# Nineteen pairs of input projections as Strassen pairs behind the head, with z and half of the conv branch kept in DRAM

## The chip, the cores and the metric

The kernel runs on one core of a Trainium2 chip. The metric is the device time of one execution in microseconds. Five engines work beside each other, each on its own list of instructions: TensorE (PE, matmuls), VectorE (DVE), ScalarE (ACT), GpSimd (POOL) and SyncE (SP, which issues loads). ACT and POOL issue DMAs too.

## The reference

One layer of a hybrid trunk over 1024 frames of width 1024, in float32: a modulated norm, one input projection that feeds a short-convolution branch, a Mamba-2 branch and the branch gates, then a squared-ReLU MLP and a final norm. Cut to what the change touches:

```python
u = rms_norm(x, ln1) * (1 + scale1) + shift1       # scale, shift, gate: (silu(c) @ w_ada + b_ada)
gl, cb, cc, cx, z, xbc, dt = split(u @ w_in)       # 2048, 3 x 1024, 2048, 4096, 32 columns
p_conv = (cb * causal_conv(cc * cx, conv_w)) @ w_conv_out            # 3 taps
xs, bs, cs = split(silu(causal_conv(xbc, ssm_conv_w) + ssm_conv_b))  # 4 taps
dt = softplus(dt + dt_bias); a = -exp(a_log) * dt
y = ssd_scan(xs * dt, a, bs, cs) + d_skip * xs     # within a chunk: scores * exp(a_cum[t] - a_cum[s]), s <= t
y = group_rms_norm(y * silu(z)) * ssm_norm_w       # 8 groups of 256 channels
mix = (sigmoid(gl0) * p_conv + sigmoid(gl1) * (y @ w_ssm_out)) @ w_o
x = x + gate1 * mix
u2 = rms_norm(x, ln2) * (1 + scale2) + shift2
x = x + gate2 * (square(relu(u2 @ w_up)) @ w_down)
return rms_norm(x, final_norm)
```

## The kernel before, in words

Everything is kept transposed: channels on 128 partitions, the 1024 frames in two halves of 512 columns. A float32 product is made of three matmuls in a rounded float type: the weight tile is split into `whi` (ACT, L87) and `wlo` (DVE, L41), the activations likewise (`uh`, `ul`), and `mm3` adds hi x hi, hi x lo and lo x hi. `proj` makes one tile of 128 output channels: 8 blocks of the inner dimension x 2 halves x 3 = 48 matmuls of 128x512, in two of the four banks of PSUM in pool `mm`. `strassen_pair` makes two tiles at once by seven half-size products, 84 matmuls; it needs sums of quarters of the activations (`tops`, T1 to T4) and of the weights (`s12`, `s34` on DVE), and holds all four banks.

The stages in order:
- the head: the norm of x, the first products with w_ada (`gemv`, one custom DVE instruction over 128x1024 and a short read), and the first four gate tiles, as the parts of u come
- gate tiles 4 to 15 (`gl`, sent to `gl_d` in DRAM) by `proj`, with the remaining 32 products with w_ada (`wada2`, loaded by SP into four buffers) on DVE beside them, and the dt block: 32 matmuls with `wd`, a chain of some 25 small operations on DVE (softplus as a series, the names `ev`, `den`, `z2`) and the cumulative sums `acum` by matmuls with `tri`
- eight groups: `proj_group(g)` makes four xbc tiles (two `xs`, `bf`, `cf`, each with a causal convolution of four taps in `cacc` on DVE) and two z tiles; `ssd_group(g)` runs the scan over eight chunks of 128 frames. A chunk has four transposes and scores (A), the decay `seg` (on DVE: subtract and min, then ACT's Exp), the products B, and the state C. After the last chunk POOL multiplies `xs` by `zs` and stores it to `y_d`, and the sum of squares goes through a split (`sqh`, `sql`) to a matmul (again named C) and a row copy
- the conv branch: eight times c, x and b tiles by `proj`, and three taps
- the products with w_conv_out, w_ssm_out and w_o, the second norm, and up: four tiles by `proj`, fourteen Strassen pairs, each hid tile stored to `hid_d`
- down: hid tiles are read back on POOL's queue (`hr`), split, and multiplied.

The order on each engine is set when the program is built: a scheduler places the instructions by their dependences, the buffers of the pools (`mm` four banks, `cacc` and `raw` two each, two sets `p2g` of xs, bf, cf) and the order of the code. An engine then runs its list in that order, and waits on semaphores where the list says so.

Of the kernel before, what the change touches and what calls it, by code (L numbers as in the profile page):

```python
# [35 lines left out]
def hybrid_trunk(tc, xT, par, hrows, crow, wada1, wada2, win, wdt, wco, wso, wo, wup, wdn, out):  # L36
# [188 lines left out]
    hb = d0.tile([P, 32], F32, name="hb")  # L225

    with tc.tile_pool(name="p0", bufs=2) as p0, tc.tile_pool(name="p0x", bufs=1) as p0x, \
            tc.tile_pool(name="ps0", bufs=2, space=PSUM) as ps0:
# [8 lines left out]
        sp.dma_start(prm, par)
        for h in (0, 1):
            ps = mm.tile([P, H], F32, name="mm")
            pe.matmul(ps, lhsT=ones[0:1, :], rhs=crw[:, hs[h]], start=True, stop=True)  # L240
            act.activation(ct[:, hs[h]], ps, AF.Tanh, scale=0.5)
            stt(cb[:, hs[h]], ct[:, hs[h]], 1.0, ps, ALU.add, ALU.mult)

        xt = [[p0x.tile([P, H], F32, name=f"x{k}{h}") for h in (0, 1)] for k in range(KT)]
        wa = {}

        def load_ada(j):
            for q in (1, 0):
                wa[j, q] = p0.tile([P, T], F32, name="wada", bufs=4)
                sp.dma_start(wa[j, q], wada1[j, :, q])  # L250

        for h in (0, 1):
            for k in range(KT):
                sp.dma_start(xt[k][h], xT[k, :, hs[h]])
        load_ada(0)

        wps = mm.tile([P, H], F32, name="mm")

        def gemv(w_, o, eng):
            if eng is dve:  # L260
                dve.tensor_tensor_reduce(out=w_, in0=w_, in1=cb, scale=0.5, scalar=prm[:, BADA + o:BADA + o + 1],  # L261
                                         op0=ALU.mult, op1=ALU.add, accum_out=mcol[:, o:o + 1])
# [525 lines left out]
```

## Time and profile before

| What | Value |
|---|---|
| Time, median of 3 runs | 2224.09 us (2221.95 to 2225.82) |
| The profiled execution | 2224.57 us, its span 2222.8 us |
| Mean granted TensorE clock | 0.986 |
| Busy PE, DVE, ACT, POOL | 98%, 60%, 31%, 9% of the span |
| DMA | 249.72 MB, mean 112 GB/s |

Busy shares are of the whole span, over stages that differ. Lines of a timeline read: start in us, duration, engine, line of the code, operation, output and input with their sizes, how many in a row, and in brackets how long the engine had been idle and what ended that. L41, L44, L47, L87 and L93 are lines of small helpers (`tt`, `stt`, `tsc`, `load_w`, `split`), so that tiles and not lines tell such instructions apart.

### The profile page before, as it was taken

The numbers are of one execution on the slowest core, as the hardware profiler recorded it, in microseconds if no ns is written. First come the engines' busy times: TensorE is split into PE (matmuls) and PEld (weight loads), VectorE is DVE, ScalarE is ACT, GpSimd is POOL, SyncE is SP. The second block draws the span as 40 slices with busy tenths as digits, with TensorE's granted clock in tenths as the row PEclk, the third lists the DMA queues.
The fourth block names the chain that finished last, engine by engine and source line by source line (L and its number), as shares of the span: only waits on it lengthen the run. The fifth ranks groups of instructions, "written<-read, shape, count | busy, mean of one in ns | idle before, by whom it ended". The sixth has DMA issues, their size and how long they took to land.

```text
span 2222.8 us, 26082 instructions
## 1 busy us (share of the span) xinstructions
PE 2169.0 (98%) x10158; PEld 1779.9 (80%) x10158; DVE 1332.8 (60%) x2195; ACT 693.9 (31%) x1044; POOL 189.4 (9%) x208
## 2 busy tenths in 40 slices
PE   5899999999999999999999999999999998999998
PEld 3778888888888888888888878888888886888887
DVE  8951368768678877574323477746755545544444
ACT  4322223333334333232111211234544443211122
POOL 5100001010110101101000000021000001000003
PEclk6999999999999999999999999999999999999999
DMA  7763222222222222231114475453233337332202
GB/s 248 269 236 116 76 57 65 79 72 71 76 59 82 77 68 84 62 83 58 49 48 154 154 231 171 152 199 109 90 110 108 114 114 256 103 109 92 86 29 77
DMA packets 105070, 249.72 MB, mean 112 GB/s; under 512 B 9281, under 2 KB 44481, under 8 KB 104946
## 3 DMA queue, kind: packets, MB, share of 16 engines
q1 hardware_dynamic: 86866, 191.22, 27.0%
q0 software_dynamic: 11584, 41.95, 5.1%
q10 hardware_dynamic: 6496, 14.88, 2.1%
q8 instruction: 80, 1.31, 0.2%
q14 instruction: 44, 0.36, 0.1%
HBM read 205.87 MB, written 42.14 MB: 112 GB/s over the span
## 4 chain that ended last, share of the span: by engine, by line
PE 80%; issue 12%; DVE 5%; DMA 2%; POOL 1%; ACT 0%; SPq 0%; POOLq 0%; DVEq 0%
PE mm L105 24%; PE mm L102 24%; PE mm L103 24%; PE B L469 2%; PE B L474 2%; DVE x L44 1%; PE C L491 1%; DVE wada L261 1%; POOL hid_d L668 1%; PE A L446 1%; DMA wada<-in_wada 1%; DVE ul L44 1%; DMA yr<-y_d 0%; PE st L190 0%; PE A L447 0%
## 5 line engine op out<-in xcount | busy, mean ns | idle before, releaser
L103 PE MATMUL mm<-ul,whi 128*128 128x512 f32 x1376 | 543.4, 395 | 4.8 <-DVE ul L44 4.6
L102 PE MATMUL mm<-uh,whi 128*128 128x512 f32 x1376 | 541.4, 394 | 0.0
L105 PE MATMUL mm<-uh,wlo 128*128 128x512 f32 x1376 | 438.0, 395 | 6.5 <-DVE wlo L41 6.5
L87 ACT CAST whi<-wraw 128x1024 fp32r<-128x1024 f32 x164 | 172.4, 1052 | 687.0 <-PE mm L103 638.7
L41 DVE TENSOR_TENSOR wlo<-wraw,whi 128x1024 fp32r<-128x1024 f32 (+1 forms) x188 | 229.2, 1219 | 178.5 <-ACT whi L87 175.2
L105 PEld LDWEIGHTS mm<-uh,wlo 128*128 128x128 f32 x1376 | 259.0, 189 | 61.1 <-DVE wlo L41 6.9
L103 PEld LDWEIGHTS mm<-ul,whi 128*128 128x128 f32 x1376 | 259.7, 189 | 59.0 <-DVE ul L44 5.6
L102 PEld LDWEIGHTS mm<-uh,whi 128*128 128x128 f32 x1376 | 259.4, 189 | 54.0 <-ACT uh L97 1.0
L102 PE MATMUL mm<-hid,whi 128*128 128x512 f32 (+1 forms) x544 | 204.1, 379 | 8.2 <-ACT hid L93 8.2
L103 PE MATMUL mm<-hid,whi 128*128 128x512 f32 (+1 forms) x544 | 204.5, 378 | 0.0
L44 DVE SCALAR_TENSOR_TENSOR y<-mm,mcol,y 128x512 f32<-128x512 f32 (+1 forms) x136 | 93.0, 716 | 167.5 <-PE mm L105 167.4
L105 PE MATMUL mm<-hid,wlo 128*128 128x512 f32 (+1 forms) x544 | 171.6, 377 | 0.0
L125 PE MATMUL mm<-s,whi 128*128 128x512 f32 x448 | 138.1, 389 | 0.7 <-ACT cu L148 0.7
L44 DVE SCALAR_TENSOR_TENSOR cacc<-raw,hw,cacc 128x1024 f32<-128x1024 f32 x96 | 128.7, 1343 | 2.2
L102 PEld LDWEIGHTS mm<-hid,whi 128*128 128x128 f32 x544 | 102.8, 189 | 27.5 <-ACT hid L93 8.6
L103 PEld LDWEIGHTS mm<-hid,whi 128*128 128x128 f32 x544 | 102.7, 189 | 19.1 <-issue 0.2
L105 PEld LDWEIGHTS mm<-hid,wlo 128*128 128x128 f32 x544 | 102.7, 189 | 19.0 <-issue 0.2
L125 PE MATMUL mm<-t,whi 128*128 128x512 f32 x336 | 103.2, 389 | 0.0
L102 PE MATMUL mm<-ys,whi 128*128 128x512 f32 x256 | 99.8, 393 | 2.8 <-DVE gt L44 2.8
L103 PE MATMUL mm<-ys,whi 128*128 128x512 f32 x256 | 99.8, 392 | 0.0
L125 PEld LDWEIGHTS mm<-s,whi 128*128 128x128 f32 x448 | 84.0, 188 | 18.6 <-ACT cu L148 1.1
L125 PE MATMUL mm<-s,wlo 128*128 128x512 f32 x224 | 87.1, 389 | 0.0
(236 smaller groups left out, 3159.8 us busy)
## 6 DMA issues: line engine op xcount, KB each, us to landing
wraw<-in_win SPq DMA_DIRECT2D x88, 512.0 KB, 3.9
wada<-in_wada SPq DMA_DIRECT2D x48, 512.0 KB, 5.0
gt<-gl_d SPq DMA_DIRECT2D x40, 512.0 KB, 3.7
acb<-ac_d SPq DMA_DIRECT2D x64, 256.0 KB, 4.7
wraw<-in_wup SPq DMA_DIRECT2D x32, 512.0 KB, 3.6
wraw<-in_wdn SPq DMA_DIRECT2D x32, 512.0 KB, 3.6
hr<-hid_d POOLq DMA_DIRECT2D x32, 512.0 KB, 4.7
hid_d<-hid POOLq DMA_DIRECT2D x28, 512.0 KB, 3.3
```

The source lines that it names most:

```text
L41: return eng.tensor_tensor(out=o, in0=a, in1=b, op=op)
L44: return dve.scalar_tensor_tensor(out=o, in0=a, scalar=s, in1=b, op0=op0, op1=op1)
L87: act.copy(hi, raw)
L102: pe.matmul(o, lhsT=wh, rhs=h_, start=start, stop=False)
L103: pe.matmul(o, lhsT=wh, rhs=l_, start=False, stop=False)
L105: pe.matmul(o, lhsT=wl, rhs=h_, start=False, stop=stop)
L125: pe.matmul(o, lhsT=l_[:, s_], rhs=r_, start=first and k == j == 0, stop=k == 3 and j == 2, skip_group_check=True)
L261: dve.tensor_tensor_reduce(out=w_, in0=w_, in1=cb, scale=0.5, scalar=prm[:, BADA + o:BADA + o + 1], op0=ALU.mult, op1=ALU.add, accum_out=m ...
L446: pe.matmul(A[:, 0:P], lhsT=bf[:, cs], rhs=cf[:, cs], start=True, stop=True)
L469: pe.matmul(Bk[o:o + 64, P * (r // 2):P * (r // 2) + P], lhsT=xd[:, r, :], rhs=seg[:, r, :], start=True, stop=True, skip_group_check=True)
L474: pe.matmul(Bk[:, 256 + P * q:256 + P * q + P], lhsT=state[:, 2 * q:2 * q + 2, :].rearrange("p r k -> p (r k)"), rhs=cf[:, cs], start=True ...
L491: pe.matmul(C, lhsT=bt, rhs=xe.rearrange("p r k -> p (r k)"), start=True, stop=True)
```

## The change

It makes 38 of the input projection's tiles by `strassen_pair` in a stage of its own behind the head: gate tiles 6 to 15 (five pairs), all z tiles (eight pairs, with silu, sent to `z_d` in DRAM), and conv f = 0 to 3 (four pairs of c and x, two of b, with their taps, sent to `yc_d`). The tops of u are built in the head; the dt block follows gate tiles 4 and 5. The 32 wada2 products go along with the pairs, three each, loaded on POOL's queue into one buffer (`wv`). `proj_group` then has four tiles. The first tap of the xbc convolution is made by ACT straight from PSUM, as is the first tap of the short convolution (`act.mul`); `seg` becomes ACT's Relu with bias, and Exp with scale -1. z is read back by SP before POOL's product. The conv stage runs f = 4 to 7 and then reads the other four back. In down, the first two hid tiles are loaded before the last up pair.

```diff
+    for k in range(4):                              # at the end of the head
+        tks.append(tc.alloc_tile_pool(name=f"tk{k}", bufs=1, side="right", reuse_waits="tile"))
+        for i, t in zip((0, 1, 2, 3), tops_of(xt[k] + xt[k + 4], mcol[:, 4 + k:5 + k], dc1[:, k:k + 1])):
+            o = [tks[-1].tile([P, H], F32R, name=f"t{i}{j}") for j in (0, 1)]
+            split(*o, t)
...
+    for f in (4, 5):
+        gl_evac(f, proj(ws[f - 4], uh, ul))
...
-        for f in range(4, 16):
-            gl_evac(f, proj(load_w(win[f]), uh, ul))
-            for i in range(3 * (f - 4), min(3 * (f - 4) + 3, 32)):
-                w_ = p0.tile([P, T], F32, name="wada", bufs=4)
-                sp.dma_start(w_, wada2[i])
-                gemv(w_, 16 + i, dve)
+    def gemvs(n):
+        for _, i in zip(range(n), gem):
+            w_ = pe1.tile([P, T + 32], F32, name="wv", bufs=1)[:, 0:T]
+            pool.dma_start(w_, wada2[i])
+            gemv(w_, 16 + i, dve)
+    for f in range(6, 16, 2):
...
+        gemvs(3)
+        strassen_pair(pe1, win[f], win[f + 1], X, gl_ev)
+        for i in (0, 1):
+            act.dma_start(gl_d[f + i], ts_[i])
+    for g in range(NG):
...
+        gemvs(3)
+        strassen_pair(pe1, win[gtile(g) + 4], win[gtile(g) + 5], X, z_ev)
+        for i in (0, 1):
+            act.dma_start(z_d[2 * g + i], ts_[i])
...
+    for f0 in range(0, NYE, 2):                     # c and x as a pair, taps, then two b as a pair
...
         for h in (0, 1):
             act.copy(raw[:, 3 + H * h:3 + H * h + H], ps[h])
         a = p2t.tile([P, T], F32, name="cacc")
-        tsc(a, raw[:, 3:3 + T], hw[:, 4 * ci + 3:4 * ci + 4], hb[:, ci:ci + 1], ALU.mult, ALU.add)
+        for h in (0, 1):
+            act.activation(a[:, hs[h]], ps[h], AF.Identity, bias=hb[:, ci:ci + 1], scale=hw[:, 4 * ci + 3:4 * ci + 4])
...
-                tsc(seg[:, r, :], acb[:, r, :], acum[:, c, hd:hd + 1], 0.0, ALU.subtract, ALU.min)
-            act.activation(seg, seg, AF.Exp)
+                act.activation(seg[:, r, :], acb[:, r, :], AF.Relu, bias=acum[:, c, hd:hd + 1], scale=-1.0)
+            act.activation(seg, seg, AF.Exp, scale=-1.0)
...
+        zs = [p2.tile([P, T], F32, name="zs") for _ in (0, 1)]
         for q in (0, 1):
-            tt(xs[:, q, :], xs[:, q, :], zs[:, q, :], ALU.mult, eng=pool)
+            sp.dma_start(zs[q], z_d[2 * g + q])
+            tt(xs[:, q, :], xs[:, q, :], zs[q], ALU.mult, eng=pool)
...
-    for f in range(8):
+    for f in [*range(NYE, 8), *range(NYE)]:
         ccs = p3.tile([P, T], F32, name="ccs")
+        if f < NYE:
+            sp.dma_start(ccs, yc_d[f])
...
+        if f == 30:
+            hrs = [load_hid(i) for i in range(2)]
```

What it does to the order shows at three places. The first is PE at the end of a group of the scan: the last chunk's B, the next groups' scores A (`A_5942` is a chunk of the next group), the sums of squares (C from `sqh` and `sql`) and projection tiles (mm). Before, around the second sum of group 2:

```order
L102 MATMUL mm_3911<-uh20_97,whi_3907 128x512
L103 MATMUL mm_3911<-ul20_113,whi_3907 128x512
L102 MATMUL mm_3912<-uh21_98,whi_3907 128x512
L103 MATMUL mm_3912<-ul21_114,whi_3907 128x512
L510 MATMUL C_3092<-sqh_3087,onec_73 128x512 [waits Activation_49]
L511 MATMUL C_3092<-sql_3088,onec_73 128x512 [waits DVE_49]
L105 MATMUL mm_3911<-uh20_97,wlo_3909 128x512
L105 MATMUL mm_3912<-uh21_98,wlo_3909 128x512
```

And now, from the last B of group 2 on; `mm_6805` is the first tile of group 5:

```order
L566 MATMUL B_5502<-seg_5495,xd_5493 64x128 [waits DVE_49,PE_49]
L566 MATMUL B_5502<-seg_5495,xd_5493 64x128 x3
L571 MATMUL B_5502<-cf_4926,state_5481 128x128 x2
L543 MATMUL A_5942<-cf_5550,bf_5549 128x128 [waits DVE_49]
L544 MATMUL A_5942<-ident_70,xs_5548 128x128
L545 MATMUL A_5942<-ident_70,xs_5548 128x128
L546 MATMUL A_5942<-ident_70,bf_5549 128x128
L609 MATMUL C_5533<-sqh_5528,onec_73 128x512 [waits Activation_49]
L610 MATMUL C_5533<-sql_5529,onec_73 128x512 [waits DVE_49]
L609 MATMUL C_5543<-sqh_5538,onec_73 128x512 [waits Activation_49]
L106 MATMUL mm_6805<-uh00_96,whi_6801 128x512 [waits Activation_49]
L107 MATMUL mm_6805<-ul00_112,whi_6801 128x512
```

Before, projection matmuls stand on both sides of the sums; now none stands between the last B and the sums, and the first projection behind them waits for ACT. ACT at the same place, before (`raw` copies of the next tile right behind the row copy of the sum):

```order
L503 ACTIVATE zs_2360<-xs_2361 128x1024 [waits Pool_49]
L457 COPY bt_3533<-A_3524 128x128 [waits DVE_49,PE_49]
L93 CAST sqh_3077<-zs_2360 128x512 [waits Pool_49]
L93 CAST sqh_3087<-zs_2360 128x512 [waits DVE_49,PE_49]
L512 COPY row_3081<-C_3082 1x512 [waits PE_49]
L513 DMA ssq_d_86<-row_3081 1x512 [waits Activation_49]
L413 COPY raw_3894<-mm_3844 128x512 [waits PE_49]
L413 COPY raw_3894<-mm_3845 128x512 [waits PE_49]
L87 CAST whi_4108<-wraw_4106 128x1024 [waits DMAHW7_49]
L512 COPY row_3091<-C_3092 1x512 [waits DMAHW3_49,PE_49]
```

And now, where `xs_6172` is group 4's buffer, the same as that of group 2, `mm_6317` the bank of group 4's bf tile:

```order
L602 ACTIVATE zs_5517<-xs_4924 128x1024 [waits Pool_49]
L602 ACTIVATE zs_5518<-xs_4924 128x1024 [waits DMAHW7_49,Pool_49]
L97 CAST sqh_5528<-zs_5517 128x512 [waits Pool_49]
L521 ACTIVATE xs_6172<-cacc_6235 128x1024 [waits DMASW5_49,DMASW4_49,Activation_49]
L521 ACTIVATE xs_6172<-cacc_6303 128x1024
L97 CAST sqh_5538<-zs_5517 128x512 [waits DVE_49,PE_49]
L611 COPY row_5532<-C_5533 1x512 [waits DMAHW1_49,PE_49]
L518 ACTIVATE cacc_6371<-mm_6317,hb_136,hw_135 128x512 [waits DVE_49]
L518 ACTIVATE cacc_6371<-mm_6318,hb_136,hw_135 128x512
```

The reading of the bank of bf (cacc from mm) now stands behind the squares, the split, two tanh that wait for DMAs, and the row copy. The second place is PE in the dt block: from the matmuls with `sel` to those with `tri`. Before, the end of it:

```order
L105 MATMUL mm_1064<-uh11_96,wlo_1061 128x512
L102 MATMUL mm_1063<-uh20_97,whi_1059 128x512
L103 MATMUL mm_1063<-ul20_113,whi_1059 128x512
L102 MATMUL mm_1064<-uh21_98,whi_1059 128x512
L371 MATMUL st_756<-z2_731,tri_71 128x256 [waits DVE_49]
L374 MATMUL st_759<-z2_731,strict_754 128x256 [waits PE_49]
L375 MATMUL st_759<-z2_731,ones_72 128x256
L103 MATMUL mm_1064<-ul21_114,whi_1059 128x512
L105 MATMUL mm_1063<-uh20_97,wlo_1061 128x512
```

And now:

```order
L140 MATMUL mm_1040<-ul30_118,whi_1048 128x512
L140 MATMUL mm_1040<-uh30_102,wlo_1050 128x512
L378 MATMUL st_956<-sel_954,dtT_917 128x32 [waits Activation_49]
L378 MATMUL st_956<-sel_954,dtT_917 128x32 x3
L410 MATMUL st_999<-z2_974,tri_71 128x256 [waits DVE_49]
L413 MATMUL st_1002<-z2_974,strict_997 128x256 [waits PE_49]
L414 MATMUL st_1002<-z2_974,ones_72 128x256
L422 MATMUL st_1009<-ident_70,acum_133 32x128 [waits Activation_49]
L422 MATMUL st_1009<-ident_70,acum_133 32x128 x3
L422 MATMUL st_1015<-ident_70,acum_133 32x128 [waits Activation_49]
L422 MATMUL st_1015<-ident_70,acum_133 32x128 x3
L140 MATMUL mm_1040<-uh40_104,whi_1048 128x512 [waits Activation_49]
```

Between the `sel` matmuls and `tri`, where 146 gate matmuls stood before, now stands nothing; the first pair (L140) goes on behind it. The third place is PE at the end of the scan, group 7, before:

```order
L102 MATMUL mm_8315<-uh31_100,whi_8310 128x512
L103 MATMUL mm_8315<-ul31_116,whi_8310 128x512
L105 MATMUL mm_8314<-uh30_99,wlo_8312 128x512
L105 MATMUL mm_8315<-uh31_100,wlo_8312 128x512
L510 MATMUL C_7514<-sqh_7509,onec_73 128x512 [waits Activation_49]
L511 MATMUL C_7514<-sql_7510,onec_73 128x512 [waits DVE_49]
L102 MATMUL mm_8314<-uh40_101,whi_8310 128x512
L103 MATMUL mm_8314<-ul40_117,whi_8310 128x512
L102 MATMUL mm_8315<-uh41_102,whi_8310 128x512
L103 MATMUL mm_8315<-ul41_118,whi_8310 128x512
```

And now, from the last chunk but one to f = 6's b tile:

```order
L566 MATMUL B_8584<-seg_8577,xd_8571 64x128 [waits DVE_49,PE_49]
L566 MATMUL B_8584<-seg_8577,xd_8571 64x128 x3
L571 MATMUL B_8584<-cf_8046,state_8559 128x128 x2
L566 MATMUL B_8622<-seg_8615,xd_8613 64x128 [waits DVE_49,PE_49,Activation_49]
L566 MATMUL B_8622<-seg_8615,xd_8613 64x128 [waits Activation_49] x3
L571 MATMUL B_8622<-cf_8046,state_8601 128x128 x2
L609 MATMUL C_8653<-sqh_8648,onec_73 128x512 [waits Activation_49]
L610 MATMUL C_8653<-sql_8649,onec_73 128x512 [waits DVE_49]
L609 MATMUL C_8663<-sqh_8658,onec_73 128x512 [waits Activation_49]
L610 MATMUL C_8663<-sql_8659,onec_73 128x512 [waits DVE_49]
L106 MATMUL mm_9210<-uh00_96,whi_9206 128x512 [waits Activation_49]
```

The last chunks and both sums of squares stand behind each other now, with no projection between them.

More of the change, by code (lines that the diff above doesn't have):

```diff
@@ new lines, in hybrid_trunk @@
+    ps0 = tc.alloc_tile_pool(name="ps0", bufs=2, space=PSUM)
+    cb = cbp.tile([P, T], F32, name="cb")
+    ct = glp.tile([P, T], F32, name="ct", tag="glt")
+    dve.memset(ones, 1.0)
+    dve.tensor_copy(onec, ones)
+    make_identity(nc, ident)
+    make_upper_triangular(nc, tri, val=1.0, diag=True)
+    crw = glp.tile([1, T], F32, name="crw", tag="glt")
+    sp.dma_start(crw, crow)
+    sp.dma_start(prm, par)
+    for h in (0, 1):
+        ps = mm.tile([P, H], F32, name="mm")
+        pe.matmul(ps, lhsT=ones[0:1, :], rhs=crw[:, hs[h]], start=True, stop=True)
+        act.activation(ct[:, hs[h]], ps, AF.Tanh, scale=0.5)
+        stt(cb[:, hs[h]], ct[:, hs[h]], 1.0, ps, ALU.add, ALU.mult)
@@ new lines, in hybrid_trunk @@
+    rbs, sts = [], []
+    for h in (0, 1):
+        st = Stats(p0, ps0, pool if h else dve, 6 if h else 8, h)
+        for k in range(KT):
+            st.add(xt[k][h])
+        rb = p0x.tile([P, H], F32, name=f"rb{h}")
+        act.copy(rb, st.rb)
+        rbs.append(rb)
+        sts.append(st)
+        if h == 0:
+            for _ in range(WARM):
+                pe.matmul(wps, lhsT=ones, rhs=xt[0][0], start=True, stop=True)
+    ws = []
+    sps = [[None, None] for _ in range(4)]
+    for h in (0, 1):
+        for f in range(4):
+            pl, nm = (mm, "mm") if f < 2 else (ps0, ("sx", "st")[h])
+            sps[f][h] = pl.tile([P, H], F32, name=nm)
@@ new lines, in hybrid_trunk @@
+    tt(wd[:, :, NH:2 * NH], wdr, wd[:, :, 0:NH].bitcast(F32), ALU.subtract)
+    dtT = p0d.tile([2 * NH, T], F32, name="dtT", tag="dact")
+    for h in (0, 1):
+        ps = ps0.tile([P, H], F32, name="st")
+        for k in range(KT):
+            pe.matmul(ps[:2 * NH], lhsT=wd[:, k, :], rhs=uh[k][h], start=k == 0, stop=False)
+            pe.matmul(ps[:2 * NH], lhsT=wd[:, k, :], rhs=ul[k][h], start=False, stop=k == KT - 1)
+        act.copy(dtT[:, hs[h]], ps[:2 * NH])
+    sel = p0d.tile([2 * NH, NH], F32, name="sel")
@@ new lines, in hybrid_trunk, with sm, as3 @@
+    tt(sel, ident[:2 * NH, 0:NH], ident[:2 * NH, NH:2 * NH], ALU.add)
+    ps = ps0.tile([P, H], F32, name="st")
+    for c in range(NC_):
+        pe.matmul(ps[:, c * NH:c * NH + NH], lhsT=dtT[:, c * P:c * P + P], rhs=sel, start=True, stop=True)
+    C2 = NC_ * NH
+    def sm(name):
+        return p0d.tile([P, C2], F32, name=name)
+    def as3(a):
+        return a.rearrange("p (c h) -> p c h", c=NC_)
+    v = sm("v")
+    tt(as3(v), as3(ps[:, :C2]), dtb.unsqueeze(1).broadcast_to([P, NC_, NH]), ALU.add)
@@ new lines, in hybrid_trunk @@
+    ev = sm("ev")
+    act.activation(ev, v, AF.Abs)
+    act.activation(ev, ev, AF.Exp, scale=-1.0)
+    den = sm("den")
+    tsc(den, ev, 2.0, None, ALU.add, ALU.bypass)
+    dve.reciprocal(den, den)
+    tt(ev, ev, den, ALU.mult)
+    z2 = sm("z2")
+    tt(z2, ev, ev, ALU.mult)
+    tsc(den, z2, 2.0 / 19.0, 2.0 / 17.0, ALU.mult, ALU.add)
+    for n in (15, 13, 11, 9, 7, 5, 3, 1):
+        tt(den, den, z2, ALU.mult)
+        tsc(den, den, 2.0 / n, None, ALU.add, ALU.bypass)
+    tt(den, den, ev, ALU.mult)
@@ new lines, in hybrid_trunk @@
+    dtf = dt_t.rearrange("p c h -> p (c h)")
+    stt(dtf, v, 0.0, den, ALU.max, ALU.add)
+    act.activation(alg, alg, AF.Exp)
+    stt(as3(z2), dt_t, -1.0, alg.unsqueeze(1).broadcast_to([P, NC_, NH]), ALU.mult, ALU.mult)
+    strict = p0d.tile([P, P], F32, name="strict")
+    tsc(strict, tri, -1.0, 1.0, ALU.mult, ALU.add)
+    ps = ps0.tile([P, H], F32, name="st")
+    pe.matmul(ps[:, :C2], lhsT=tri, rhs=z2, start=True, stop=True)
+    act.copy(acum.rearrange("p c h -> p (c h)"), ps[:, :C2])
```

368 lines of the change are left out of this document (179 added, 189 removed).

## The prediction

> **What bounds the kernel now.** I read the page's table of engines first, then busy time by stretch, then the chain of waits, and last the timelines of all engines at the places where the change takes cover away. The first line is the table of engines; the other two are stretches of the scan and of the up stage (length, then busy us of PE, of its weight loads, of DVE, ACT and POOL, the granted clock, the DMA share, GB/s).
>
> ```profile
> PE 2169.0 (98%) x10158; PEld 1779.9 (80%) x10158; DVE 1332.8 (60%) x2195; ACT 693.9 (31%) x1044; POOL 189.4 (9%) x208
> ...
> 403.00:843.00 440.00, 440.00 (x2289) 358.78 (x2288) 343.78 (x692) 161.94 (x285) 40.02 (x43) 1.00 0.25 72
> ...
> 1676.00:1733.00 57.00, 57.00 (x254) 47.19 (x253) 30.13 (x39) 27.57 (x39) 3.07 (x7) 1.00 0.32 111
> ```
>
> TensorE is busy in all 440 us of the scan and in all 57 of the up stage, DVE in 78% and 53%, ACT in 37% and 48%. So a matmul that goes is worth its time on PE, and a wait that PE gets is paid in full. Two paces of PE, as ACT's casts of weights (they wait for PE's tile) and as the chain of waits show them (start, length, what):
>
> ```profile
> 144.23 1.06 ACT L87 CAST whi<-wraw 128x1024 fp32r<-128x1024 f32 x1 [8.85 <-PE mm L103]
> ...
> 155.11 1.05 ACT L87 CAST whi<-wraw 128x1024 fp32r<-128x1024 f32 x1 [8.85 <-PE mm L103]
> ...
> 1676.19 15.78 issue
> ...
> 1695.24 15.77 issue
> ```
>
> A direct tile of 48 matmuls takes 155.11 - 144.23 = 10.88 us, 0.2267 us for each. A Strassen pair of the up stage takes 19.05 us, which is its 84 matmuls at the same 0.2268. A pair is therefore 2.72 us shorter than two direct tiles while its operands are ready. Where PE has waited, it is slow afterwards (in brackets: idle time before, and what ended it):
>
> ```profile
> 101.47 1.22 PE L105 MATMUL mm<-uh,wlo 128*128 128x512 f32 x2 [6.49 <-DVE wlo L41]
> ...
> 105.05 0.44 PE L102 MATMUL mm<-uh,whi 128*128 128x512 f32 x1
> ...
> 1844.84 6.90 DMA hr<-hid_d
> ...
> 1852.87 2.08 PE L102 MATMUL mm<-hid,whi 128*128 128x512 f32 x4 [8.20 <-ACT hid L93]
> ...
> 1857.25 1.09 PE L102 MATMUL mm<-hid,whi 128*128 128x512 f32 x4
> ```
>
> The eight matmuls from 101.47 to 105.05 take 3.58 us after a wait of 6.49, where eight at full pace take 1.81; four take 2.08 us after a wait of 8.20 and 1.09 later. I add 1.8 us to each long wait as its cold start.
>
> **The pairs.** 19 pairs save 12 matmuls each: 228 x 0.2267 = 51.7 us off PE, if nothing waits. Their tops (32 half-tile operations on DVE, as many splits) are made at the end of the head in the place of five wada2 products, and wlo of the first gate tile, which came behind ten products there, now comes behind 19 half-tile operations; the wait of 6.49 us above stays. I count 0, between -3 and +3.
>
> **The group boundaries of the scan.** This is the largest term. The rows are one boundary of the kernel before, PE's last B and the first of two A's, DVE's last chunk, POOL's products with z and their stores, POOL's sum of squares, ACT's and DVE's split of it, the row copy, and a tanh, its stt and a raw copy from other places.
>
> ```profile
> 471.86 0.71 PE L474 MATMUL B<-cf,state 128*128 128x128 f32 x4
> 476.08 0.38 PE L446 MATMUL A<-cf,bf 128*128 128x128 f32 x2
> 476.63 0.39 PE L446 MATMUL A<-cf,bf 128*128 128x128 f32 x2
> 472.61 0.42 DVE L41 TENSOR_TENSOR t<-B,ebc 128x256 f32<-128x256 f32 x1 [5.39 <-PE B L474]
> 473.53 0.61 DVE L44 SCALAR_TENSOR_TENSOR xs<-xs,prm,t 128x128 f32<-128x128 f32 x2
> 473.96 4.79 POOL L41 TENSOR_TENSOR xs<-xs,zs 128x1024 f32<-128x1024 f32 x2 [14.09 <-DVE xs L44]
> 478.69 1.12 POOL L502 DMA_DIRECT2D y_d<-xs  x2
> 480.00 2.39 POOL L41 TENSOR_TENSOR zs<-zs 128x1024 f32<-128x1024 f32 x1 [0.19 <-ACT zs L503]
> 482.43 0.62 ACT L93 CAST sqh<-zs 128x512 fp32r<-128x512 f32 x1 [1.71 <-POOL zs L41]
> 483.08 0.69 DVE L41 TENSOR_TENSOR sql<-zs,sqh 128x512 fp32r<-128x512 f32 x1 [0.86 <-ACT sqh L93]
> 488.56 0.57 ACT L512 COPY row<-C 1x512 f32<-1x512 f32 x1
> 459.66 1.06 ACT L418 ACTIVATE cf<-cacc 128x1024 f32<-128x1024 f32 x1 [3.09 <-DVE cacc L44]
> 460.75 1.23 DVE L44 SCALAR_TENSOR_TENSOR cf<-cf,cacc 128x1024 f32<-128x1024 f32 x1 [0.60 <-ACT cf L418]
> 489.71 1.08 ACT L413 COPY raw<-mm 128x512 f32<-128x512 f32 x2 [0.57 <-PE mm L105]
> DMA to landing us min/median/max: 3.0/3.4/6.1
> ```
>
> The chain from the end of B (472.57) to the end of the split's cast (483.05) is 10.5 us, and the y_d stores, issued at 478.69 and 479.25, land at about 482.4. In the kernel before PE covers it with tiles whose banks are free (440 of 440 us busy). In the changed order nothing is left to cover it: at the boundaries after groups 1 to 5 PE has already run all four tiles of the group after next, so that bf and cf hold all four mm banks. The bank that the next tile wants is released by ACT's first tap (L518), which stands behind two tanh into xs (they wait for the y_d stores, since xs(g+2) is xs(g)'s buffer), the second split's cast and the row copy. With the durations above (tanh 1.06, cast 0.62, copy 0.57, and for the half-tile tap 0.54 as raw's copy): 10.5 + 1.06 + 1.06 + 0.62 + 0.57 + 0.54 = 14.4 us after B. The first stt on xs (1.23), which frees the cacc buffer, ends at 10.5 + 1.06 + 1.23 = 12.8 and is hidden. Meanwhile PE has one chunk's A (476.63 - 476.08 = 0.55) and three sums of 0.23, 1.25 us; after group 1 it has 2.8. Idle: 4 x 13.1 + 11.6 = 64.0 us, plus five cold starts, 73.0. The lower bound is 8 us each (an ACT that does the row copy and the tanh while it waits for DVE), the upper 16. I take the sum of rows, since each of them is the same instruction on the same tile. After groups 0 and 6 the order has 50 matmuls and more there, and I count nothing.
>
> **The tail of the scan.** In group 7 only the eight direct conv tiles before f=6's b are left as cover, and they are used up before the last four chunks. Per chunk, from the groups of DVE (count | busy, mean ns):
>
> ```profile
> L41 DVE TENSOR_TENSOR seg<-seg,smk 128x512 f32<-128x512 f32 x39 | 26.2, 681 | 3.4 <-ACT seg L464 3.4
> ...
> L41 DVE TENSOR_TENSOR state<-C,state 128x256 f32<-128x256 f32 x48 | 19.8, 413 | 0.4 <-PE C L491 0.3
> ```
>
> DVE has 0.68 for seg, six operations of 128x256 (t twice, xd, xe, state twice) at 0.41 and the two stt at 0.61 together, some 3.5 us with what overlaps, against 1.45 of PE's own B and C (estimated from its 0.71 above): 2.05 idle for each of three chunks, 6.2. Then the whole chain of squares to its second half: 10.5 + 0.69 + 0.5 of matmuls + 0.62 + 0.69 + 0.4 = 13.4, less 0.9 of PE's own, 12.5. Then f=6's b wants the bank that ACT empties after the row copy and four casts of yc: 0.57 + 4 x 0.62 + 0.54 = 3.6. With one cold start 24.1; between 12 and 32.
>
> **The dt block.** Rows of PE (sel), DVE and ACT:
>
> ```profile
> 124.53 1.08 PE L339 MATMUL st<-sel,dtT 64*128 64x32 f32 x8
> ...
> 125.64 0.42 DVE L41 TENSOR_TENSOR v<-st,dtb 128x256 f32<-128x256 f32 x1 [2.63 <-PE st L339]
> ...
> 126.55 0.42 ACT L352 ACTIVATE ev<-ev 128x256 f32<-128x256 f32 x1
> ...
> 128.59 1.75 DVE L355 RECIPROCAL den<-den 128x256 f32<-128x256 f32 x1
> ...
> 141.48 0.42 DVE L41 TENSOR_TENSOR den<-den,z 128x256 f32<-128x256 f32 x1
> ...
> 142.26 0.43 DVE L41 TENSOR_TENSOR den<-den,z 128x256 f32<-128x256 f32 x1
> ```
>
> A pair of den operations takes 142.26 - 141.48 = 0.78 us, 0.46 for the product and 0.32 for the sum. Alone on DVE the chain to z2 is v 0.46, two activations 0.95, den 0.32, reciprocal 1.75, two products 0.92, den 0.32, eight pairs 6.24 and three more 1.38: 12.3 us. Before, gate tiles ran on PE meanwhile. Now tri's matmul (L410) stands directly behind sel's on PE, with the first pair behind it: 12.5 idle + 1.8 = 14.3, between 9 and 17.
>
> **The 32 products of wada2** move into the pairs, three a pair, over one buffer, loaded on POOL's queue (they came by SP into four). The nearest loads of POOL and the product:
>
> ```profile
> 98.98 1.28 DVE L261 CUSTOM_DVE_ANT_0 wada<-wada,cb,prm 128x1024 f32<-128x1024 f32 x1 [1.94 <-DMA wada<-in_wada]
> ...
> L668 POOL DMA_DIRECT2D hid_d<-hid x28 | 14.9, 532 | 251.8 <-ACT hid L664 251.8
> ...
> hr<-hid_d POOLq DMA_DIRECT2D x32, 512.0 KB, 4.7
> ```
>
> Each round is 0.5 issue + 4.7 landing + 1.36 on DVE = 6.6, three are 19.7 us against a pair's 19.05. DVE then carries 10.0 (30.13 / 3) + 4.1 a pair, and four half-tile products more in a z pair: under 17. Of the 0.65 x 10.7 = 7 us that this falls behind, about half is taken by the slack of DVE ahead of PE: +4, between 0 and 30 (at 5.7 to landing). The row on hid_d has 0.53 us an issue in a stage where DVE is 53% busy: nothing holds POOL's issue up there. The Trainium skill (SBUF — State Buffer, "SBUF: two separate sides") has a rule against this move: a DMA from GpSimd's queue waits while VectorE runs an operation that locks their shared port, 3100 ns instead of 620. By it each of the 32 loads could take some 2.5 us more, an estimate from that page of up to 80 us; the row of hid_d does not bear it out.
>
> **What is costed at nothing.** The clamp goes from DVE (279 ns) to ACT, 256 times:
>
> ```profile
> L47 DVE TENSOR_SCALAR seg<-acb,acum 128x128 f32<-128x128 f32 x256 | 55.0, 279 | 5.7 <-DMA acb<-ac_d 3.0 <-PE C L510 1.9 <-PE C L511 0.8
> ...
> L457 ACT COPY bt<-A 128x128 f32<-128x128 f32 x56 | 14.8, 264 | 150.8 <-DVE xd L41 150.8
> ```
>
> At 0.27 by bt's copy that is 8.5 us of ACT a group. A group is now 288 projection matmuls, 65.3 us, and the scan's own 19; by the stretch above ACT has 31 of these 84 us and DVE 66. After the change PE has 192 x 0.2267 + 19 = 62.6, ACT some 40 and DVE some 48. Both stay below PE, which is why the gain of the clamp is nothing either: DVE did not bind. The conv's tap on ACT lies beside PE's tiles. The z loads on SP wait for POOL's sum of the group before (9.8 us after B), with the acb loads of the next chunks and weights queued behind them; these are a chunk and a tile ahead of their users, and I count nothing. 40 more transfers of 512 KB are small beside a DMA share of 0.25; if the yc loads came late, wco would wait some 4 us.
>
> **The early read of hid** takes the wait of 8.20 at the start of down away and its slow matmuls: -9.2, between -10 and -6, since hid 2 and 3 still follow.
>
> Sum: -51.7 + 73.0 + 24.1 + 14.3 + 4 - 9.2 = +54.5. The profiled execution took 2224.6 us, 0.5 above the median of 2224.1: 2279.
>
> **Rivals.** (a) Faster: PE finds its bank free at the boundaries. The place is the wait before the first tile after each ssq; it decides at 18.5 / 5 = 3.7 us a boundary, cold start included. Without it the sum is -18.5: 2206. For it: PE never waited there so far. Against it: a bank can't be free before ACT's tap, and ACT's tap stands behind the stores in the order. 0.11. (b) The loop of wada2 binds the pairs: loads that take 5.7 us (the 32 of hr reach 10.9) make 22.7 us a pair, 3.6 x 10.7 = 39 behind, and with 5 us of slack and the 4 counted +30: 2309. The rule of the Trainium skill quoted above would act here, in the same direction. 0.10. (c) Tail and dt block find cover (ACT and DVE ahead by more than the rows say): 54.5 - 38 = +16: 2241. 0.12. The forecast has 0.67.
>
> Numbers: 0.2% of this kernel is 4.4 us, about what a measurement can tell. Faster 0.12 (nearly all of (a) and a little of (c)), same 0.03, slower 0.85. The range takes in (c) and most of (b): 2236 to 2309.
>
> **What the changed profile would show.** Right: a wait of PE before mm (L106) ended by ACT cacc, five times at 11 to 14 us, with half the granted clock behind each; one of 12 us before st (L410) ended by DVE; a pair each 19 us between them; PE's share under 95%; no wait over 2 us at the start of down. Wrong: PE busy throughout 500 to 900 us; or pairs of 22 us, with DVE idle before wv ended by a DMA.

## The result and the profile after

The changed kernel takes 2294.5 us (median; 2291.1 to 2298.5), the kernel before took 2224.9 beside it: a ratio of 1.0315 [1.0295, 1.0336], slower. The forecast was 2279, in a range of 2236 to 2309.

The lines that answer to those of before: the table of engines, then two stretches, four periods of the scan between two boundaries and the stage of the pairs (length, busy us of PE, PEld, DVE, ACT, POOL, granted clock, DMA share, GB/s).

```profile
PE 2149.4 (94%) x9930; PEld 1750.0 (76%) x9930; DVE 1405.1 (61%) x2141; ACT 871.3 (38%) x1441; POOL 203.1 (9%) x240
...
742.50:1052.50 310.00, 262.61 (x1368) 207.06 (x1367) 204.56 (x384) 171.60 (x364) 33.92 (x36) 0.90 0.28 82
...
152.20:517.40 365.20, 361.51 (x1585) 296.93 (x1586) 267.09 (x370) 118.22 (x157) 17.83 (x40) 1.00 0.43 145
```

PE has less work and a smaller share. The pairs run nearly full (361.5 of 365.2 us at a clock of 1.00). In the scan, where PE was busy for all of 440 us before, it is now busy for 262.6 of 310 at a clock of 0.90: a period is 77.5 us, where the forecast had 62.6 of work for PE. PE's waits by their releasers (us in total, times, longest; the six waits for `sqh` are the five boundaries and the tail), then the first boundary on the timeline:

```profile
PE C L609 <- ACT sqh L97: 55.1, 6, 10.3
PE st L410 <- DVE z L45: 12.4, 1, 12.4
PE C L609 <- ACT row L611: 9.5, 6, 2.0
...
PE mm L140 <- ACT whi L145: 4.7, 2, 3.6
```

```profile
726.42 0.71 PE L571 MATMUL B<-cf,state 128*128 128x128 f32 x4
...
728.72 5.66 POOL L42 TENSOR_TENSOR xs<-xs,zs 128x1024 f32<-128x1024 f32 x2 [23.20 <-DVE xs L45]
...
729.27 2.92 DVE L42 TENSOR_TENSOR wlo<-wraw,whi 128x1024 fp32r<-128x1024 f32 x1 [0.37 <-ACT whi L91]
...
734.33 1.12 POOL L601 DMA_DIRECT2D y_d<-xs  x2
735.56 2.33 POOL L42 TENSOR_TENSOR zs<-zs 128x1024 f32<-128x1024 f32 x1
737.92 0.62 ACT L97 CAST sqh<-zs 128x512 fp32r<-128x512 f32 x1 [2.45 <-POOL zs L42]
738.60 0.79 PE L609 MATMUL C<-sqh,onec 128*128 128x512 f32 x1 [9.44 <-ACT sqh L97]
738.79 2.00 ACT L521 ACTIVATE xs<-cacc 128x1024 f32<-128x1024 f32 x2 [0.25 <-DMA y_d<-xs]
740.70 0.60 ACT L97 CAST sqh<-zs 128x512 fp32r<-128x512 f32 x1
741.21 0.57 ACT L611 COPY row<-C 1x512 f32<-1x512 f32 x1
741.69 0.77 ACT L518 ACTIVATE cacc<-mm,hb,hw 128x512 f32<-128x512 f32 x1
741.83 0.79 PE L609 MATMUL C<-sqh,onec 128*128 128x512 f32 x1 [1.72 <-ACT row L611]
742.51 0.80 PE L106 MATMUL mm<-uh,whi 128*128 128x512 f32 x1
...
746.52 0.63 PE L106 MATMUL mm<-uh,whi 128*128 128x512 f32 x1
...
747.32 0.40 PE L109 MATMUL mm<-uh,wlo 128*128 128x512 f32 x1
747.55 0.39 PE L106 MATMUL mm<-uh,whi 128*128 128x512 f32 x1
747.78 0.39 PE L107 MATMUL mm<-ul,whi 128*128 128x512 f32 x1
```

The last B ended at 727.13. POOL's products, their sum and ACT's cast run one after another; then come ACT's two tanh into `xs` (released by the store `y_d<-xs`), the second cast, the row copy and the first tap at 741.69, and PE goes on with a tile at 742.51, 15.4 us after B. At the four other boundaries it is 14.8 to 15.1 us. Up to 747 PE's matmuls start 0.43 us apart instead of 0.23.

The dt block, the tail of scan 7, and the first pair of the up stage (ACT's row shows what it waited for):

```profile
146.26 1.22 PE L410 MATMUL st<-z,tri 128*128 128x256 f32 x2 [12.45 <-DVE z L45]
...
1191.46 0.80 PE L609 MATMUL C<-sqh,onec 128*128 128x512 f32 x1 [10.35 <-ACT sqh L97]
...
1198.48 0.79 PE L106 MATMUL mm<-uh,whi 128*128 128x512 f32 x1 [3.62 <-ACT ccs L637]
...
1656.66 1.04 ACT L97 CAST hida<-hr 128x1024 fp32r<-128x1024 f32 x1 [4.68 <-DMA hr<-hid_d]
1657.61 1.99 ACT L145 CAST whi<-s 128x1024 fp32r<-128x1024 f32 x2
1658.70 2.93 PE L140 MATMUL mm<-t,whi 128*128 128x512 f32 x6 [3.63 <-ACT whi L145]
```

### The profile page after: what moved, and what is told of

Same layout as the page of the kernel before. It is cut to its first block, busy times and chain, and to the rows that moved or that the text cites. A ratio compares the mean times of both kernels' runs of the same rounds, so it can differ in the third digit from the quotient of the medians.

```text
span 2293.4 us, 26126 instructions
## 1 busy us (share of the span) xinstructions
PE 2149.4 (94%) x9930; PEld 1750.0 (76%) x9930; DVE 1405.1 (61%) x2141; ACT 871.3 (38%) x1441; POOL 203.1 (9%) x240
## 4 chain that ended last, share of the span: by engine, by line
PE 65%; issue 20%; DVE 7%; DMA 4%; ACT 2%; POOL 2%; SPq 0%; POOLq 0%; DVEq 0%; ACTq 0%
PE mm L106 15%; PE mm L107 15%; PE mm L109 15%; PE mm L140 15%; DMA wv<-in_wada 1%; DVE x L45 1%; DMA y_d<-xs 1%; PE B L566 1%; DMA yr<-y_d 1%; POOL xs L42 1%; DVE cacc L45 1%; PE C L588 1%; PE B L571 1%; DVE wada L280 1%; DMA hr<-hid_d 1%
## 5 line engine op out<-in xcount | busy, mean ns | idle before, releaser
L107 PE MATMUL mm<-ul,whi 128*128 128x512 f32 x768 | 311.2, 405 | 5.7 <-DVE ul L45 5.7
L106 PE MATMUL mm<-uh,whi 128*128 128x512 f32 x768 | 310.3, 407 | 5.4 <-ACT ccs L637 3.6
L140 PE MATMUL mm<-t,whi 128*128 128x512 f32 x944 | 292.2, 392 | 7.2 <-ACT whi L145 4.7
L109 PE MATMUL mm<-uh,wlo 128*128 128x512 f32 x768 | 256.0, 403 | 0.0
L140 PEld LDWEIGHTS mm<-t,whi 128*128 128x128 f32 x944 | 177.6, 189 | 47.0 <-ACT whi L145 5.7
L45 DVE SCALAR_TENSOR_TENSOR y<-mm,mcol,y 128x512 f32<-128x512 f32 (+1 forms) x136 | 92.7, 716 | 150.4 <-PE mm L109 148.9
L140 PE MATMUL mm<-t,wlo 128*128 128x512 f32 x472 | 183.3, 390 | 0.0
L106 PEld LDWEIGHTS mm<-uh,whi 128*128 128x128 f32 x768 | 149.0, 194 | 41.3 <-ACT ccs L637 4.3
L107 PEld LDWEIGHTS mm<-ul,whi 128*128 128x128 f32 x768 | 149.4, 195 | 36.1 <-DVE ul L45 6.1
L109 PEld LDWEIGHTS mm<-uh,wlo 128*128 128x128 f32 x768 | 147.4, 194 | 30.9 <-issue 0.3
L106 PE MATMUL mm<-hid,whi 128*128 128x512 f32 (+1 forms) x416 | 154.1, 374 | 0.0
L140 PE MATMUL mm<-s,whi 128*128 128x512 f32 x448 | 137.9, 389 | 0.7 <-ACT cu L163 0.7
L45 DVE SCALAR_TENSOR_TENSOR cacc<-raw,hw,cacc 128x1024 f32<-128x1024 f32 x96 | 123.6, 1301 | 15.1 <-ACT cacc L518 14.4
L560 ACT ACTIVATE seg<-acb,acum 128x128 f32<-128x128 f32 x256 | 81.8, 392 | 94.0 <-PE B L566 84.9
L106 PE MATMUL mm<-ys,whi 128*128 128x512 f32 x256 | 99.9, 393 | 3.7 <-DVE gt L45 3.7
L140 PEld LDWEIGHTS mm<-t,wlo 128*128 128x128 f32 x472 | 88.7, 188 | 18.6
L145 ACT CAST whi<-wraw 128x1024 fp32r<-128x1024 f32 x66 | 55.1, 837 | 120.0 <-PE mm L140 108.5
```

Source lines behind the costliest of these rows:

```text
L45: return dve.scalar_tensor_tensor(out=o, in0=a, scalar=s, in1=b, op0=op0, op1=op1)
L106: pe.matmul(o, lhsT=wh, rhs=h_, start=start, stop=False)
L107: pe.matmul(o, lhsT=wh, rhs=l_, start=False, stop=False)
L109: pe.matmul(o, lhsT=wl, rhs=h_, start=False, stop=stop)
L140: pe.matmul(o, lhsT=l_[:, s_], rhs=r_, start=first and k == j == 0, stop=k == 3 and j == 2, skip_group_check=True)
L145: act.copy(hi, src)
```

## The experiments

The medians, and the ratios to the kernel before, which ran beside each. Gains and losses in us below are between medians.

| kernel | us | ratio, 95% interval |
|---|---|---|
| the change | 2294.5 | 1.0315 [1.0295, 1.0336] |
| x1_xs3 | 2269.8 | 1.0204 [1.0188, 1.0219] |
| x2_ccs3 | 2286.3 | 1.0279 [1.0264, 1.0295] |
| x3_dt_cover | 2285.0 | 1.0272 [1.0257, 1.0288] |
| x4_hid_only | 2225.2 | 1.0004 [0.9994, 1.0013] |
| x5_z_direct | 2212.7 | 0.9943 [0.9928, 0.9958] |
| x6_z_dt | 2201.7 | 0.9886 [0.9870, 0.9903] |
| x7_z_dt_clamp | 2221.5 | 0.9989 [0.9978, 0.9999] |
| x8_z_dt_clamp_tap | 2228.3 | 1.0013 [1.0004, 1.0023] |
| x9_hid_held | 2197.9 | 0.9886 [0.9870, 0.9903] |
| x10_after_clamp | 2308.7 | 1.0385 [1.0369, 1.0400] |
| x11_hid_only_held | 2217.2 | 0.9970 [0.9958, 0.9981] |

**x1: is it `xs`'s buffer?**

```diff
-        xs = pg.tile([P, 2, T], F32, name="xs")       # two, one in each of p2g
+        xs = xsp.tile([P, 2, T], F32, name="xs")      # pool xsp, bufs=3
```

> The changed kernel with a third buffer for xs, so that the tanh into xs(g+2) no longer waits for group g's stores. Theory (a bank held at the group boundary): the five waits of PE of 9 us before the sums, and the cold matmuls behind them, go; a group falls from 78 to some 64 us, the whole from 2294 to about 2225 (2215 to 2240). Rival (the scan's own chain of DVE, ACT and POOL takes 75 us a group whatever the buffers are): the wait moves into the chunks of the next groups, and the time stays above 2265.

Measured: -24.7 us, the rival. The longest waits of PE in the scan, and what is left of those for `sqh`, are now these:

```profile
PE B L567 <- DVE t L42: 14.7, 13, 2.2
...
PE mm L106 <- ACT ccs L638: 9.0, 2, 5.5
PE A L544 <- DVE xe L42: 8.7, 7, 2.8
PE mm L106 <- ACT cacc L519: 5.6, 2, 5.3
...
PE C L610 <- ACT sqh L97: 3.3, 1, 3.3
```

The waits for `sqh` went from 55.1 to 3.3, but those inside the chunks grew: before B for DVE's `t` from 3.4 to 14.7 us, before A for `xe` from 6.3 to 8.7. All of PE's idle time from 500 to 1250 us fell from 78 to 54. With the third buffer the order has 28 to 83 tile matmuls between the last B of groups 1 to 6 and the first sum of squares; the changed kernel has 5 there after group 1 and none after groups 2 to 5. So the buffer sets where PE waits, and about a third of how long. That the rest is PE having too few matmuls for the scan's chain is what x5 tests.

**x2: a third `ccs` for the tail.** `ccs = p3.tile(..., name="ccs", bufs=3)`.

> The changed kernel with three instead of two buffers ccs in the conv stage. Theory (nothing covers group 7's tail because f = 6's b has no buffer): the order puts more conv tiles between the last chunks, PE's waits of 10.4 and 3.6 us and the small ones before B go; 20 to 25 us faster, about 2271. Rival (ACT and DVE are behind there anyway): under 8 us faster.

Measured: -8.2, at the rival's edge. The wait of 10.35 in the tail is down to 1.20, but the next one, `PE mm L106 <- ACT ccs L637`, is 5.3 us (3.6 in the changed kernel): six casts of `yc` stand ahead of ACT's evacuation there, 3.21 us, where the changed kernel has four, 2.18.

**x3: cover for the dt block.** Gates 4 to 7 as direct tiles behind sel's matmuls.

```diff
-    for f in (4, 5):                                  # ahead of the dt block
-        gl_evac(f, proj(ws[f - 4], uh, ul))
+    for f in range(4, 8):                             # behind sel's matmuls
+        gl_evac(f, proj(ws[f - 4] if f < 6 else load_w(win[f]), uh, ul))
-    for f in range(6, 16, 2):
+    for f in range(8, 16, 2):
```

> The changed kernel with gate tiles 4 to 7 by direct projection, written after the sel matmuls (one Strassen pair fewer, 2.7 us more of PE). Theory (the dt chain is uncovered): the wait of 12.4 us before tri and its cold matmuls go; 17 - 3 = 14 us faster (11 to 17), about 2280. Rival (the first pair's s12, which comes behind the dt chain on DVE, is what PE really waits for): 0 to 5 us faster.

Measured: -9.6, just under the range. The wait of 12.45 is gone altogether. Behind the dt block this kernel goes on with its pair of gates 8 and 9 at 159.6 us. The changed kernel goes on with gates 6 and 7 at 152.2 and reaches that point of gates 8 and 9 a pair of some 19 us later, so this kernel is some 12 us ahead there. PE's wait of 1.65 for `cu` behind the dt block is here too (1.69). Why 9.6 and not 12 us are left at the end is not shown.

**x4: the early hid read alone, in the kernel before.** With it come the buffers of the change: two of `hr` in place of three, and two for the early tiles beside six others in place of eight.

> The kernel before with only the early read of two hid tiles. Theory: the wait of 8.2 us at the start of down and its cold matmuls go, 9 to 10 us faster, about 2215. Rival (the time is given back in down, as the changed kernel's new wait of 2.3 us before an early down tile suggests): 5 us or less.

Measured: no gain. The wait of 8.20 at the start of down is gone, and two others are there (DVE's y, and the weights of the first pair of up):

```profile
1584.47 1.04 ACT L93 CAST hida<-hr 128x1024 fp32r<-128x1024 f32 x1 [5.01 <-DMA hr<-hid_d]
1585.42 1.99 ACT L130 CAST whi<-s 128x1024 fp32r<-128x1024 f32 x2
...
1586.52 2.17 PE L125 MATMUL mm<-t,whi 128*128 128x512 f32 x6 [3.98 <-ACT whi L130]
...
1862.76 0.50 PE L102 MATMUL mm<-hida,whi 128*128 128x512 f32 x1 [2.31 <-DVE y L44]
```

The loads and casts of the two early tiles stand at the start of up and not at f = 30: POOL issues the loads at 1578.3, right behind a store to `hid_d` at 1577.7. ACT's cast then waits 5.0 us for `hr`, and behind it stand the casts that PE's first pair needs.

**x5: z back between the chunks.** The z tiles as direct tiles in `proj_group`, without `z_d`; gates 6 to 15 and the conv tiles stay pairs, with three wada2 products each. Two smaller edits come with it: `cy` of the pairs has one buffer in place of two, and the wada2 products have a buffer of their own (`wg`).

```diff
+        for q in (0, 1):                              # in proj_group
+            ps = proj(load_w(win[b + 4 + q]), uh, ul)
+            for h in (0, 1):
+                act.activation(zs[:, q, hs[h]], ps[h], AF.Tanh, scale=0.5)
+                stt(zs[:, q, hs[h]], zs[:, q, hs[h]], 1.0, ps[h], ALU.add, ALU.mult)
```

> The changed kernel with the z tiles back as direct tiles between the scan's chunks (96 matmuls a group), so z isn't stored and read back; 5 gate pairs and 6 conv pairs stay Strassen pairs, three wada2 products in each. Of the 19 pairs 8 go: +8 x 2.72 = +21.8 us. Theory (the boundaries wait because PE has no tile left whose bank is free): the five waits of 15.4 us and the tail of scan 7 (23.5) vanish, -77 - 23.5: 2294.5 - 78.7 = 2216 us (2208 to 2226), with no wait over 2 us before ssq's matmuls. Rival (the scan's own chain over DVE and ACT is too slow for this order, as the third xs buffer let it appear inside the chunks): half or more of the 100 us stays, over 2260.

Measured: 2212.7, -81.9 against the -78.7 expected, and 0.6% faster than before the change. PE shows no wait for `sqh` at all, and is busy in all of the old stretch again:

```profile
403.00:843.00 440.00, 440.00 (x2292) 357.73 (x2292) 322.29 (x520) 233.96 (x480) 48.79 (x47) 1.00 0.25 73
```

Between the last B of a group and its first sum PE now has 72 to 76 tile matmuls. The edit also takes z's store and load away. That is not the gain: at the changed kernel's boundary POOL's product waits for DVE's `xs` (`[23.20 <-DVE xs L45]` at the first boundary) and not for z.

**x6: x5 with x3's edit.** One pair fewer, so the two pairs of b have four wada2 products each.

> x5_z_direct with gates 4 to 7 as direct tiles behind sel's matmuls, as in x3_dt_cover (there -9.6 us). If the two gains add, 2216 - 9.6 = 2206 us (2197 to 2217), which is faster than before the change. If the cover only moves the waits, 2216 or over.

Measured: 2201.7, -11.0 against x5: the gains add. It is 1.1% faster than before the change.

**x7 and x8: clamp and tap back on DVE, where PE is covered.**

```diff
-                act.activation(seg[:, r, :], acb[:, r, :], AF.Relu, bias=acum[:, c, hd:hd + 1], scale=-1.0)
+                tsc(seg[:, r, :], acb[:, r, :], acum[:, c, hd:hd + 1], 0.0, ALU.subtract, ALU.min)
...
-            act.activation(a[:, hs[h]], ps[h], AF.Identity, bias=hb[:, ci:ci + 1], scale=hw[:, 4 * ci + 3:4 * ci + 4])
+        tsc(a, raw[:, 3:3 + T], hw[:, 4 * ci + 3:4 * ci + 4], hb[:, ci:ci + 1], ALU.mult, ALU.add)   # x8 only
```

> x6_z_dt with the clamp back on DVE (256 operations of 279 ns there, four Relu of 0.32 to 0.39 us a chunk on ACT now). Theory: off the path where PE is covered, within 3 us of x6_z_dt. Rival 1: ACT is what the scan's chain runs through, so taking 10 us a group off ACT gains 5 us or more. Rival 2: DVE binds, so 9 us a group more on DVE cost 5 us or more.

> x7_z_dt_clamp with the conv's first tap back on DVE too (one operation on 128x1024 from raw in the place of two activations on 128x512 from the bank), so that the Strassen pairs, the dt block's cover and the early hid read alone are left of the change. Theory: the bank is released by ACT's raw copy one activation (0.55 us) earlier, hidden: within 3 us of x7_z_dt_clamp. Rival (the tap on ACT saves DVE time that binds): 5 us or more slower.

Measured: +19.8 for the clamp and +6.8 more for the tap, both outside what I called hidden. Yet PE waits nowhere in the scan before group 7; x7's waits of 1 us and more from 300 to 1200 us are these three:

```profile
1108.33 0.66 PE L561 MATMUL B<-seg,xd 128*64 128x128 f32 x8 [1.60 <-DVE t L42]
...
1119.91 0.80 PE L602 MATMUL C<-sqh,onec 128*128 128x512 f32 x1 [10.29 <-ACT sqh L97]
...
1125.58 0.80 PE L106 MATMUL mm<-uh,whi 128*128 128x512 f32 x1 [2.26 <-ACT ccs L630]
```

14.2 us of waiting and its cold matmuls are most of the 19.8; x8 adds waits before B ended by DVE's `t` (4.9 us against 1.6). In the traces x6 has run 195 or 196 tile matmuls before the last B of each of groups 1 to 6, x7 195 to 238. In group 7, x6 has 32 and 24 of them ahead of the last two B and 72 ahead of the sums; x7 has 15 and 0, and none ahead of the sums. I read this as DVE's 4 x 0.28 us a chunk having been paid for in tiles, which were then missing at the end. That is an argument from the order and no test of it: the scheduler chose that order, and the same clamp under another was not tried.

**x9: the early hid tiles held back on ACT.** x6, with

```diff
+            if b == 0 and i < 2:
+                with tc.issue_after(late[26].ins):        # the activation of up pair 26
+                    split(t[:, 0, :], t[:, 1, :], hr)
```

> x6_z_dt with the splits of the two early hid tiles held on ACT and DVE behind the activation of up pair 26 (the loads stay where they are). In x6_z_dt, as in x4_hid_only, ACT's cast of hida stands in the first up pair and waits 5.2 us there for hr, with the casts of the pair's weight sums behind it; PE then waits 4.2 us and starts cold. Theory (the gain of the early read was given back by ACT's place in the order): -6 us (-4 to -8), 2196 us, no wait of PE over 1 us in the first up pairs and none of 8 us at the start of down. Rival (the weights' own way is late there, since the pair's operands come late too): within 2 us of 2201.7.

Measured: 2197.9, 3.8 under x6 and just short of the range. The ratios, each to the kernel before beside it, are the same, so the times do not tell the two kernels apart. In the trace the wait of 4.2 us in the first up pair is gone.

**x10: the clamp back on DVE in the changed kernel.** x7's edit there.

> The changed kernel with only the clamp back on DVE. My prediction costed the clamp's move at nothing: then 2294.5 within 4 us. Theory after x7_z_dt_clamp (+19.8 there, though no wait of PE before the last group): DVE's 1.1 us more a chunk are paid in PE's tiles, some four matmuls a chunk that the order puts there as cover, so the cover of a group is spent earlier; here the last chunks of each group stand without any. Three chunks of some 3 us of DVE beyond PE's own work in each of five groups: +40 us, 2335 (2315 to 2355), with waits before B (L566) ended by DVE t or ACT seg. Between the two, +10, would speak for part of the cover being there already.

Measured: +14.1, between the two. A boundary and the chunk before it, first in this kernel, then in the changed one:

```profile
810.91 0.46 PE L543 MATMUL A<-cf,bf 128*128 128x128 f32 x2 [1.47 <-DVE xe L42]
813.77 0.49 PE L543 MATMUL A<-cf,bf 128*128 128x128 f32 x2 [0.85 <-DVE xe L42]
823.41 0.80 PE L609 MATMUL C<-sqh,onec 128*128 128x512 f32 x1 [8.82 <-ACT sqh L97]
```

```profile
806.61 0.49 PE L543 MATMUL A<-cf,bf 128*128 128x128 f32 x2 [1.26 <-DVE xe L42]
...
816.24 0.80 PE L609 MATMUL C<-sqh,onec 128*128 128x512 f32 x1 [8.81 <-ACT sqh L97]
```

The boundary's own wait is the same; one more chunk waits. Over the whole scan the waits before A for `xe` grew from 6.3 to 14.5 us and those before B for `t` from 3.4 to 5.4, while those for `sqh` stayed (55.1 and 53.8). DVE's 1.1 us in 64 chunks would be some 71 us; most of it was still covered.

**x11: x4 with x9's hold.**

> The kernel before with the early hid read alone, as in x4_hid_only (no gain there), and the splits of the two early tiles held behind the activation of up pair 26. My prediction had -9.2 us for this edit. Theory (the gain was given back by ACT's cast of hida, which waited 5.0 us for hr ahead of the casts of the first up pair): the wait of 4.0 us in the first up pair goes; of the 8.2 us wait at the start of down and its cold start a wait of 2.4 ended by DVE y and some cold matmuls stay: -6 us (-4 to -8), 2217 to 2221 us. Rival (a wait of this length costs less than it shows, since work behind it catches up): within 2 us of before.

Measured: 2217.2, -6.9, in the range; x4 without the hold gained nothing. What is left at the start of down is

```profile
1856.27 0.80 PE L102 MATMUL mm<-hida,whi 128*128 128x512 f32 x1 [2.38 <-DVE y L44]
```

DVE's evictions stand behind the split of the third hid tile there, which still comes late.

## Why the prediction was right, and where it was not

The sign and the main mechanism held; the sum was 16 us short. By the marks of the two traces the start of the product with w_conv_out came 70.5 us later (1174.5 to 1245.0), the end 70.6 later. Term by term:

- **Pairs, -51.7: held.** 1584 matmuls took 365.2 us, 6.1 over full pace.
- **Boundaries, +73.0 and tail, +24.1: held.** What is left for the whole scan when the other terms are taken off, 70.5 + 51.7 + 2.4 - 16.4 - 6.1, is 102.1 against 97.1. PE resumed 14.8 to 15.4 us after B (14.4 predicted), and the cold starts took 2.3, 2.7, 2.8, 1.4 and 2.3 us (1.8 predicted); the first is eleven matmuls from 742.51 to 747.32, 4.8 us where 2.5 are full pace. Less PE's full-pace work in between, the five boundaries come to some 79 us, an estimate from these rows, so most of the 5 us is theirs. The forecast's 62.6 of work a period hides this: the period is just its 14.9 us longer, but by the same estimate the work is nearer 61.8. The tail is some 24 us as predicted, and that is partly luck: its waits were 19.4 us against the 22.3 of the forecast, and the slow matmuls behind them cost 4.8 and not 1.8.
- **The wait's name: wrong.** PE takes its list in order, so it stands before the sums' matmuls (`C<-sqh`, 8.8 to 9.4 for the first and 1.7 to 2.0 for the second) and not before the tile whose bank ACT frees. No wait before mm ended by ACT cacc was seen, which I had given as the sign of being right. The second sum starts at 741.83, and the bank is free at 742.46: the predicted chain sets when PE gets on, and only the place of the wait is another.
- **That they wait for want of cover: shown** by x5, which puts 96 direct matmuls a group back and is within 3.3 us of its sum. Rival (a) is out. That the buffer of `xs` alone is the cause fell with x1: a freer bank was worth about a third of the 73.
- **dt block, +14.3: 16.4.** The wait was 12.45 (12.5 predicted); 1.65 for `cu` came behind it, and 2.3 for the cold start. x3 took the first and the cold start away; the wait for `cu` stayed.
- **wada2, +4: at most 6.1**, which is all that the pairs lost, and 1.05 of it is a wait for `whi` in their first. `wv` landed in 3.9 us, not 4.7, and the pairs' waits for `cq` are 0.3 to 0.7 us each. Rival (b) is out. The up to 80 us, my estimate from the Trainium skill (SBUF — State Buffer, "SBUF: two separate sides") for loads from GpSimd's queue that wait on VectorE, did not come, though DVE was busy for 267 of 365 us there. This is no test of that rule: the 3100 ns of the Trainium skill are beside a DVE `tensor_copy`, and the trace has none in this stretch.
- **Head, 0 within 3: -2.4**, by the start of the first gate tile's 18th matmul (105.78 before, 103.39 after). The size held and the reason did not: the wait of 6.49 that I had left as it was is down to two of 1.03 and 0.76, but the head's own matmuls ended 2.1 us later.
- **Early hid, -9.2: the step that failed; it was worth nothing.** I took the loads to stand where the code has them, and looked at the stage's end only. They and the casts stand at the start of up, and ACT's cast waited there for a DMA with PE's weights behind it (x4; x11 brings 6.9 back). In the sum this is the largest error, 9 of the 16 us. The sign "no wait over 2 us at the start of down" missed a little too: one of 2.28 for DVE's `y` is there.
- **Clamp and tap, 0.** For the sum this did no harm, I think because it was read from the changed order, in which their gain is already spent. As a statement on the operations it was wrong: +14.1 (x10) and +19.8 (x7) without the clamp, +6.8 (x8) without the tap. The Relu took ACT 0.32 us each (81.8 us for 256), not the 0.27 of `bt`'s copy that I took, and ACT was still the better place in these orders.
- **Rival (c), cover for tail and dt, is out**: PE waited 12.45 us before `tri` and 19.4 in the tail.

x6 and x9 (2201.7 and 2197.9) beat both kernels: the gate and conv pairs, the clamp and the tap on ACT and a covered dt block, with z left in the scan.

## What to carry to other kernels

Where an engine is busy all the time, ask first what else its work was covering: eight z pairs saved 22 us of matmuls and cost about 100 in waits and slow matmuls, because those matmuls were what the scan ran behind. An operation beside the path can have a price too when an order is planned around it: as the orders of x6 and x7 suggest, it was paid in tiles in the early groups and in a wait of PE in the last one. An early load helped here only when its first user was held back as well (x4 against x11); on an engine that takes its list in order, a cast that waits for a DMA stops everything behind it.

## What the runs showed of the hardware

After the first boundary (9.4 us idle, two matmuls, 1.7 idle) PE ran eleven matmuls of 128x512, 4.8 us, at half pace; the granted clock was 0.51 from 742.5 to 747.3 and 1.00 behind it. At the other four it was 13, 13, 6 and 11 matmuls. A Relu of 128x128 with a bias on ACT has a mean of 0.39 us in the records and costs 0.32 in a row of four, since they overlap. POOL's two products of 128x1024 took 4.68 to 4.80 us at most group ends and 5.66 to 5.78 at four: at the first boundary of the changed kernel and after groups 0, 3 and 4 of the kernel before. At each of these four, and at no other, an operation of DVE on 128x1024 started during POOL's first product, and it was slowed as well: `wlo` to 2.92 us at that boundary, where it takes 1.23 alone.
